# Chunked attention heads: the second copy of a query page's high half by a DMA from SP instead of by GpSimd

## The chip, the cores and the metric

The kernel runs on one core of a Trainium2 chip. Its engines are TensorE (PE; its weight loads are listed apart as PEld), VectorE (DVE), ScalarE (ACT), GpSimd (POOL) and SyncE (SP). Each runs its own list of instructions in order; semaphores order the lists against each other. In this kernel every DMA is issued by SP. The metric is the device time of one execution in microseconds.

## What is computed

One layer of a streaming encoder on a sequence of 1024 rows of width 1024, in float32:

```python
mod = silu(c) @ w_ada + b_ada                       # six rows of 1024: shift, scale, gate, twice
h = rmsnorm(x, g_attn_norm) * (1 + sc_a) + sh_a
proj = h @ w_in                                     # 416 latent columns, then q, k, v of 8 chunked heads
o_mla = latent attention, 8 heads, chunk-causal     # from the 416 columns
cq, ck, cv = rmsnorm(q), rmsnorm(k), v              # 8 heads of 64 columns
o_ca: each chunk of 64 queries sees its own and the 8 chunks before it;
      s = cq @ ck.T / 8 + rel_bias[clip(distance)]; softmax(s) @ cv
x = x + g_a * (concat(o_mla, o_ca) @ w_out)
h = rmsnorm(x, g_mlp_norm) * (1 + sc_m) + sh_m
gate, val = split(causal_dwconv(h @ w_up))
x = x + g_m * ((silu(gate) * val) @ w_down)
```

The change lies in `o_ca`, where the queries `cq` are brought into the form in which TensorE reads them.

## The kernel before

The 1024 rows are eight tiles of 128. To keep float32 accuracy on TensorE, an operand is split into a high part (rounded to fp32r) and a low part (what the rounding left), and a product is made from three matmuls: high by high, high by low and low by high.

The work goes in stages: the conditioning and the first projection (to about 85 us of the trace), the chunked heads together with the rest of the projections (to about 290 us, its last tiles to about 340), the latent heads (to about 600), the output projection, and the channel sub-layer, in which TensorE is busy with the up and down projections to the end.

The eight chunked heads come as four pairs p. A head pair's normalized queries and keys lie beside each other in a tile `qn` (128 rows, two heads of 64 query columns, two heads of 64 key columns). They are worked in two groups g of 512 queries, and in each group the two heads o follow each other, four query tiles of 128 each. So there are eight pages (p, g), each used by eight query tiles, and 64 query tiles in all.

`ca_pages(p, g)` makes a query page and a key page. TensorE transposes four blocks of `qn` into one PSUM bank (`page_psum`, L749): rows 0 to 63 hold head 0, rows 64 to 127 head 1. For each head o, ACT copies its 64 rows as the high part into `qp` (`qh[o]`, L781), DVE writes the low part into `qlow` (L782), and POOL copies the high part once more into the other 64 rows of the same tile (L783). The key page `kp` has the high part of the keys in head o's rows and their low part in the other 64 rows (L787 on ACT, L788 on DVE). One matmul over all 128 rows (L822 in `Unit.scores`) then makes high by high and high by low at once, and a second, with `qlow`, low by high. That is why the high part of the queries is needed twice.

`qfix[g]` holds two tiles (one for each head) for each group, so a page of pair p + 1 overwrites the tiles of the same group of pair p. The transposed queries and keys share one PSUM bank with one buffer: the key page is transposed after the query page has been read out.

A page is prepared two query tiles before its first use (the loop over `tiles`, `v.prep()`), where the projections it needs are done; else right before. The page of (p, o = 0) serves both heads: `ca_pages` runs once for a (p, g), and the tile of head 1 is used four query tiles after that of head 0.

A query tile goes through `scores` (TensorE, then DVE adds the bias and takes the row extreme, then ACT's exponential at L854, `Pc`), a normalization into two float16 halves `hlc` (POOL at L74 the high one, DVE at L876 the low one, both with the reciprocal `ric` from DVE), a DMA transpose issued by SP (L888, into `PTc`), and `values` (TensorE at L916). SP's list also holds the loads of weights (`wq_r`, `wv_r`, `wm_r` at L195, `aw` at L447), of biases (L946), and the stores of the output (`oT_d` at L930).

Between the attention tiles, TensorE is given steps of the other projections ("fillers"), paced by reckoned cost. The splits of those weights are on ACT (L78) and POOL (L85), and the normalization of the next pair's queries and keys (`qk_norm`: L350 to L357) ends on POOL with `qn`. The order of each engine's list is in the end set by a planner, which goes through the program with its own durations of each instruction and with priorities: scores, normalization and values are raised by fixed offsets (`OFF_S`, `OFF_P`, `OFF_V`). `issue_after` pins an instruction behind another on the same engine.

Of the kernel before, what the change touches and what calls it, by code (L numbers as in the profile page):

```python
# [65 lines left out]
def layer_kernel(ctx, tc, I, out):  # L66
    nc = tc.nc
    pe, act, dve, pool, sp = nc.tensor, nc.scalar, nc.vector, nc.gpsimd, nc.sync

    def f32(ap):  # L70
        return ap.bitcast(F32)
# [211 lines left out]
    for d in range(ND):  # L283
        dd, half = divmod(d, 2)
# [460 lines left out]
    def page_psum(src, name, rows, tag="T"):  # L745
        pt = ps.tile([P, 512], F32, name=f"{name}_ps", tag=tag, bufs=TB)
        with tc.issue_after(first[0]):
            for j in range(4):
                pe.transpose(pt[:rows, j * P:(j + 1) * P], src(j), ident[:])  # L749
        return pt  # L750
# [20 lines left out]
    def ca_pages(p, g):  # L771

        qn = qns[p, g]
        half = (slice(0, 64), slice(64, 128))
        pt = page_psum(lambda j: qn[:, j, 0:128], f"q{p}_{g}", P)
        if p == g == 0:
            pk_ = page_psum(lambda j: qn[:, j, 128:256], f"k{p}_{g}", P, "pv")
        qh = qfix[g]
        ql = qlow[0], qlow[1 + g]
        for o in range(2):  # L780
            act.activation(qh[o][half[o]], pt[half[o]], AF.Copy)  # L781
            dve.tensor_tensor(ql[o][half[o]], pt[half[o]], f32(qh[o][half[o]]), op=SUB)  # L782
            pool.tensor_copy(qh[o][half[1 - o]], f32(qh[o][half[o]]))  # L783
        pt = pk_ if p == g == 0 else page_psum(lambda j: qn[:, j, 128:256], f"k{p}_{g}", P)
        kk = kfix[(2 * p + g) % 3]
        for o in range(2):
            act.activation(kk[half[o], o], pt[half[o]], AF.Copy, scale=gk_ca[half[o]])  # L787
            dve.scalar_tensor_tensor(kk[half[1 - o], o], pt[half[o]], gk_ca[half[o]], f32(kk[half[o], o]),  # L788
                                     op0=MUL, op1=SUB)
        return (qh, ql), kk  # L790
# [165 lines left out]
    def ca_unit(p, g, o):  # L956
        def prep():
            if (p, g, o) == (0, 0, 0):
                load_bias(0)
            if g == 0 and o == 0:  # L960
                load_bias(2 * p + 1)
            if g == 1 and o == 0 and p < 3:
                load_bias(2 * p + 2)
            if g == 0:
                mask_bias(2 * p + o)
            if o == 0:
                pages["c", p, g] = ca_pages(p, g)
        u = Unit(f"c{p}{o}", 64 * o, 64,
                 lambda: (pages["c", p, g][0], [pages["c", p, i][1] for i in range(g + 1)]),
                 lambda j: vts[p][:, j, o].rearrange("p a b -> p (a b)"),  # L970
                 g, True, lambda: biases[2 * p + o], o, oT_d[4 + p], ("c", p // 2))
        u.prep = prep
        u.need = [f"qk{p}"] if p else []
        u.needv = [f"v{p // 2}"]
        return u
# [623 lines left out]
    for t in range(4):  # L1599
        o = dl.tile([P, 512], F32, name=f"oe{t}", tag="oe", bufs=3)  # L1600
# [80 lines left out]
```

## Time and profile before

| | |
|---|---|
| median of 3 runs | 1311.97 us (1311.38 to 1319.53) |
| the profiled execution | 1312.59 us, of which the trace's span is 1310.8 us |
| PE busy | 1189.1 us (91%) |
| DVE busy | 1075.0 us (82%) |
| ACT busy | 625.8 us (48%) |
| POOL busy | 597.9 us (46%) |
| all DMA of the program | 190.82 MB, mean 146 GB/s |

Busy times are of one execution under the profiler. A row of a group of instructions gives line, engine, operation, output and inputs by the names in the program, shape and count, then busy time and mean duration, then the idle time of that engine just before them and what ended it. A row of the timeline gives start, length, engine, line, operation, and in brackets the idle time before and its releaser; neighbours of one kind are merged with their count. Waits are rows "who waited <- for whom: us in total, times, longest". For a DMA, the duration is that of the issue on SP, and the time to landing is given apart. Idle time of an engine that isn't the bottleneck costs nothing by itself.

### The profile page before, as it was taken

Reading aid. Unit: us, or ns where it says so; the run is one execution under the profiler, and the core shown is the slowest. Engines: PE = TensorE matmul, PEld = TensorE weight load, DVE = VectorE, ACT = ScalarE, POOL = GpSimd, SP = SyncE. Lnnn points to the kernel's source line nnn. Section 1 sums busy time; section 2 is a strip of 40 time slices with the busy share of each in tenths; the row PEclk is TensorE's granted clock in tenths of the full one; section 3 lists DMA queues with packets and bytes.
Section 4 is the critical chain, followed back from the end, with each engine's and each line's share of the span. In section 5 each row is a group of like instructions: output and inputs, shape, how many; then the busy total and the mean of one; then the engine's idle time right before and its main releaser. Section 6 shows DMA issues by size and latency. Waiting matters only on the chain. (4 is left out here: it accounts for less than half of the span.)

```text
span 1310.8 us, 18660 instructions
## 1 busy us (share of the span) xinstructions
PE 1189.1 (91%) x6168; PEld 988.0 (75%) x6168; DVE 1075.0 (82%) x1800; ACT 625.8 (48%) x1148; POOL 597.9 (46%) x639
## 2 busy tenths in 40 slices
PE   3899998889767889878989999999999999999998
PEld 3789888878545667656778888888888886888886
DVE  6979988888589778875899889888888987687667
ACT  5454654455567454543474443444453353433331
POOL 5485773587688534445515444544445441000000
PEclk9899999989889998988999999999999999999999
DMA  8416758766224777679503333343333337943451
GB/s 323 150 50 154 177 141 189 158 161 123 51 70 85 161 162 149 147 161 357 231 0 112 97 125 116 119 128 107 105 121 111 122 105 267 395 135 102 129 161 64
DMA packets 223688, 190.82 MB, mean 146 GB/s; under 512 B 148708, under 2 KB 166372, under 8 KB 223592
## 3 DMA queue, kind: packets, MB, share of 16 engines
q1 hardware_dynamic: 223592, 189.64, 51.4%
q8 instruction: 48, 0.79, 0.3%
q14 instruction: 48, 0.39, 0.1%
HBM read 117.50 MB, written 37.49 MB: 118 GB/s over the span
## 5 line engine op out<-in xcount | busy, mean ns | idle before, releaser
L78 ACT ACTIVATE dnP<-dnr 128x1024 fp32r<-128x1024 f32 x73 | 77.5, 1065 | 116.3 <-PE dnA_P L1492 46.3
L1464 DVE TENSOR_TENSOR dnP<-dnr,dnP 128x1024 fp32r<-128x1024 f32 x72 | 88.3, 1230 | 51.3 <-ACT dnP L78 51.3
L74 POOL TENSOR_SCALAR hlm<-Pm,rim 128x512 f16<-128x512 f32 (+3 forms) x96 | 67.5, 712 | 73.4 <-DVE rim L857 20.2
L85 POOL TENSOR_TENSOR wf<-wu,wf 128x512 fp32r<-128x512 f32 x22 | 39.6, 1798 | 116.6 <-ACT wf L78 116.6
L85 POOL TENSOR_TENSOR wb<-wu,wb 128x512 fp32r<-128x512 f32 x22 | 43.8, 1993 | 84.8 <-ACT wb L78 57.1
L876 DVE SCALAR_TENSOR_TENSOR hlm<-Pm,rim,hlm 128x512 f16<-128x512 f32 (+3 forms) x96 | 72.3, 769 | 12.4 <-POOL hlm L74 12.1
L829 PE MATMUL sm<-kp,qp 96*128 96x512 f32 (+7 forms) x288 | 70.0, 370 | 10.8 <-ACT Pm L854 7.7
L1326 DVE SCALAR_TENSOR_TENSOR u<-c,cvp,u 128x1023 f32<-128x1023 f32 x44 | 55.8, 1310 | 27.6 <-ACT u L1325 26.2
L854 ACT ACTIVATE Pm<-sm,mm 128x128 f32<-128x128 f32 (+3 forms) x64 | 47.3, 740 | 44.7 <-DVE mm L847 35.4
L74 POOL TENSOR_SCALAR hlc<-Pc,ric 128x640 f16<-128x640 f32 (+2 forms) x64 | 48.8, 765 | 42.8 <-DVE ric L857 14.7
L854 ACT ACTIVATE Pc<-sc,mc 128x640 f32<-128x640 f32 (+2 forms) x64 | 42.3, 662 | 51.4 <-DVE mc L844 28.6
L829 PEld LDWEIGHTS sm<-kp,qp 96*128 96x128 f32 (+1 forms) x288 | 48.0, 195 | 21.9 <-ACT Pm L854 12.3
L1325 ACT ACTIVATE u<-c,cvp 128x1024 f32<-128x1024 f32 x44 | 52.4, 1240 | 23.4 <-DVE c L1424 16.5
L916 PE MATMUL pvm<-PTm,vt 128*128 128x256 f16 (+1 forms) x320 | 42.6, 279 | 19.7 <-DMA PTm<-hlm 17.1
L876 DVE SCALAR_TENSOR_TENSOR hlc<-Pc,ric,hlc 128x640 f16<-128x640 f32 (+2 forms) x64 | 52.5, 827 | 8.5 <-POOL hlc L74 8.3
L78 ACT ACTIVATE wc<-ws 128x512 fp32r<-128x512 f32 x21 | 13.3, 634 | 92.9 <-DVE ws L1174 87.1
L1327 DVE SCALAR_TENSOR_TENSOR u<-c,cvp,u 128x1022 f32<-128x1022 f32 x44 | 55.5, 1302 | 0.0
L155 PE MATMUL ipq<-wq_s,hT 128*128 128x256 f32 x192 | 55.5, 289 | 0.0
L916 PEld LDWEIGHTS <-vt 128*128 128x128 f16 x320 | 30.1, 103 | 33.3 <-issue 20.5
L157 PE MATMUL ipq<-wq_s,hT 128*128 128x256 f32 x192 | 54.6, 284 | 0.0
L156 PE MATMUL ipq<-wq_s,hT 128*128 128x256 f32 x192 | 54.6, 284 | 0.0
L1491 PE MATMUL dnA_P<-dnP 128*128 128x512 f32 x132 | 51.3, 389 | 0.0
(436 smaller groups left out, 4376.0 us busy)
## 6 DMA issues: line engine op xcount, KB each, us to landing
wu<-w_up SPq DMA_DIRECT2D x44, 512.0 KB, 3.6
dnr<-g_d SPq DMA_DIRECT2D x73, 256.0 KB, 2.8
aw<-w_ada SPq DMA_DIRECT2D x48, 256.0 KB, 3.2
g_d<-u SPq DMA_DIRECT2D x22, 512.0 KB, 3.0
dnr<-w_down SPq DMA_DIRECT2D x44, 256.0 KB, 5.4
adaw<-w_ada_a SPq DMA_DIRECT2D x16, 512.0 KB, 6.4
x<-x SPq DMA_DIRECT2D x16, 512.0 KB, 9.1
g_d<-gs SPq DMA_DIRECT2D x22, 256.0 KB, 2.8
```

The lines of the kernel that those rows point to most:

```text
L74: pool.tensor_scalar(o, i, s, 1.0, op0=MUL, op1=MUL)
L78: act.activation(o, i, AF.Copy)
L85: (pool if eng == "p" else dve).tensor_tensor(o, i, f32(hi), op=SUB)
L155: pe.matmul(pt, sh, mh, start=(start and i == 0), stop=False)
L156: pe.matmul(pt, sh, ml, start=False, stop=False)
L829: last = pe.matmul(s[:, c:c + w], qpg[a][rr, q], kpgs[kh][rr, b, ko:ko + w], start=(a == 0 and b == 0), stop=(a == 1))
L854: act.activation(pr[:, :n], sv, AF.Exp, bias=m[:], scale=-1.0, accum_out=rsum[:, 0:1])
L876: dve.scalar_tensor_tensor(hl[:, w:2 * w], pp, ri[:], hl[:, :w], op0=MUL, op1=SUB)
L916: last = pe.matmul(dst, u.vst(j), mov, start=(x == 0), stop=(x == len(todo) - 1), skip_group_check=True)
L1326: dve.scalar_tensor_tensor(u[:, 1:], c[:, :S - 1], cvp[:, cv + 1:cv + 2], u[:, 1:], op0=MUL, op1=ADD)
L1327: dve.scalar_tensor_tensor(u[:, 2:], c[:, :S - 2], cvp[:, cv:cv + 1], u[:, 2:], op0=MUL, op1=ADD)
L1464: r = f(*a, **k)
```

## The change

For seven of the eight pages, the copy of the high part into the other 64 rows is a DMA within SBUF, issued by SP. The first page (p = 0, g = 0) keeps POOL's copy. Source, destination and bytes are the same: 64 rows of 512 float32, 128 KB. There are two copies for each page, so 14 instructions leave POOL's list and 14 DMAs come into SP's.

```diff
         for o in range(2):
             act.activation(qh[o][half[o]], pt[half[o]], AF.Copy)
             dve.tensor_tensor(ql[o][half[o]], pt[half[o]], f32(qh[o][half[o]]), op=SUB)
-            pool.tensor_copy(qh[o][half[1 - o]], f32(qh[o][half[o]]))
+            if p == g == 0:
+                pool.tensor_copy(qh[o][half[1 - o]], f32(qh[o][half[o]]))
+            else:
+                sp.dma_start(f32(qh[o][half[1 - o]]), f32(qh[o][half[o]]))
```

## The prediction

> **What bounds the kernel now.** I read the page's busy table first, then a table of windows by stage, then what TensorE (PE) waited for in the stage that the change touches.
>
> ```profile
> span 1310.8 us, 18660 instructions
> PE 1189.1 (91%) x6168; PEld 988.0 (75%) x6168; DVE 1075.0 (82%) x1800; ACT 625.8 (48%) x1148; POOL 597.9 (46%) x639
> 85.00:290.00 205.00, 183.69 (x1386) 170.47 (x1386) 182.00 (x516) 108.27 (x268) 131.06 (x169) 0.97 0.68 159
> 290.00:600.00 310.00, 254.56 (x1364) 200.25 (x1363) 240.54 (x558) 167.33 (x401) 186.69 (x252) 0.92 0.61 129
> 750.00:1310.00 560.00, 551.66 (x2403) 451.35 (x2401) 457.19 (x458) 231.88 (x288) 160.52 (x106) 0.99 0.43 141
> ```
>
> The last three rows are start:end, length, then busy time and count of PE, PE's weight loads, DVE, ACT and POOL, then granted clock, DMA share and GB/s. After 750 us PE is nearly full (551.66 of 560) and nothing of this change reaches it. The copies of the change stand between 85 and 290 us: there PE is busy 183.69 of 205 and DVE 182.00, so two engines are close to the limit and POOL, with 131.06, is not. PE leaves 205 - 183.69 = 21.3 us idle in that stage; this is all that the change could win there. Who took it:
>
> ```profile
> PE pvc L916 <- DMA PTc<-hlc: 9.6, 7, 2.5
> PE sc L822 <- ACT Pc L854: 7.4, 6, 2.7
> ```
>
> (us in total, times, longest.) PE waits for transposed probabilities, which SP's DMA queue brings, and for a score bank that ACT's exponential frees. It never waits for the POOL copy, as its own rows say:
>
> ```profile
> L783 POOL CAST qp<-qp 64x512 fp32r<-64x512 f32 x16 | 10.9, 680 | 9.8 <-ACT qp L781 9.0
> 85.20 1.28 POOL L783 CAST qp<-qp 64x512 fp32r<-64x512 f32 x2
>   POOL hlc L74: 0.2, 1
> ```
>
> The first is the group of all 16 copies (busy us, mean ns, POOL idle before them and its releaser), the second the pair that the change keeps, the third the only instruction that waited for a copy.
>
> **Removed from POOL.** 14 copies go: 10.9 - 1.28 = 9.6 us of POOL, and its 9.0 us of waiting for ACT, which all stand before the 14. Whether that is worth anything depends on what stood behind each copy:
>
> ```profile
> 142.13 0.61 POOL L783 CAST qp<-qp 64x512 fp32r<-64x512 f32 x1 [4.24 <-ACT qp L781]
> 142.97 0.84 POOL L74 TENSOR_SCALAR hlc<-Pc,ric 128x640 f16<-128x640 f32 x1 [0.23 <-POOL qp L783]
> 142.66 0.15 DVE L857 TENSOR_SCALAR ric<-ric 128x1 f32<-128x1 f32 x1
> 269.06 0.61 POOL L783 CAST qp<-qp 64x512 fp32r<-64x512 f32 x1
> 269.75 1.21 POOL L85 TENSOR_TENSOR wm_l<-wm_r,wm_h 128x160 fp32r<-128x160 f32 x2
> 271.70 1.05 POOL L357 TENSOR_TENSOR qn<-raw,r 128x512 f32<-128x512 f32 x1
> ```
>
> At the longest wait (4.24) the next POOL instruction needed DVE's `ric`, ready at 142.81, so it could start only 0.16 us sooner. At 269 the copy does stand in a chain: it holds the line up by 269.75 - 269.06 = 0.7 us, and at the end of that line is the normalization `qn` of the last rows of pair 3, which the key page of that pair is made from. PE's score there is the only one of the stage with a wait for a key page:
>
> ```profile
> 274.83 0.33 PE L822 MATMUL sc<-kp,qp 128*128 128x128 f32 x1 [0.32 <-DVE kp L788]
> ```
>
> So this copy's going is worth between 0.3 (what PE waited) and 0.7 us; I take 0.7. At the other places POOL's next work waits for ACT or DVE, or PE is full; nothing.
>
> There is also DVE. Instructions with two inputs in SBUF stretch at times:
>
> ```profile
> L461 DVE SCALAR_TENSOR_TENSOR aacc<-aw,cs,aacc x42: 674/751/1415, 114.0 to 297.4; 128x512 f32<-128x512 f32 x42
> L461 DVE SCALAR_TENSOR_TENSOR aacc<-aw,cs,aacc 128x512 f32<-128x512 f32 x39 | 33.3, 853 | 2.9 <-DMA aw<-w_ada 2.6
> ```
>
> Shortest 674 ns, mean in the stage 853: 39 x 179 ns = 7.0 us more than the shortest. If overlap with POOL does that, the copies' part of it is 9.6 of POOL's 131.06, or 0.5 us; with the other groups of two SBUF inputs I take 1.0 us. Bounds: nothing, and 14 x 0.68 = 9.5 us, if every copy blocked DVE for its whole length.
>
> The Trainium skill, page "SBUF — State Buffer", section "SBUF: two separate sides", says that VectorE instructions with two SBUF inputs and GpSimd instructions that read SBUF exclude each other for the whole instruction, and that DMA has other ports. The stretched rows agree with it without proving it; by the rule in full, DVE's gain is the upper bound just given, which is the mechanism of the faster rival below.
>
> **Added to SP.** 14 DMAs of 64 rows x 2 KB, 128 KB each. No row shows SBUF to SBUF without a transpose; the nearest is the store of attention output, also 64x512 out of SBUF and also issued by SP. Beside it the transposes that share SP:
>
> ```profile
> L930 SPq DMA_DIRECT2D oT_d<-oc x16: 451/461/667, 109.3 to 339.7; - x16
> DMA to landing us min/median/max: 2.2/2.3/3.1
> L888 SPq DMA_TRANSPOSE PTc<-hlc x64: 1167/1314/2634, 93.1 to 332.5; - x64
> DMA to landing us min/median/max: 2.4/3.4/5.6
> PTc<-hlc SPq DMA_TRANSPOSE x42, 3.4
> ```
>
> I take 0.46 us of issue and 2.3 us to landing; upper ends are the store's 0.67 of issue and the slowest transpose's 5.6. From the end of ACT's `qp` to a usable copy that is 2.8 us, at worst 6.3, where POOL needed 0.6 plus its own queue. The tightest three of the 14:
>
> ```profile
> 266.43 0.60 ACT L781 ACTIVATE qp<-q_ps 64x512 fp32r<-64x512 f32 x1
> 163.11 0.58 ACT L781 ACTIVATE qp<-q_ps 64x512 fp32r<-64x512 f32 x1
> 171.68 0.80 PE L822 MATMUL sc<-kp,qp 128*128 128x512 f32 x1
> 269.36 0.59 ACT L781 ACTIVATE qp<-q_ps 64x512 fp32r<-64x512 f32 x1
> 279.67 0.33 PE L822 MATMUL sc<-kp,qp 128*128 128x128 f32 x1
> ```
>
> Source ready to first use: 267.03 to 274.83 is 7.8 us, 163.69 to 171.68 is 8.0, 269.95 to 279.67 is 9.7; the other eleven have 13 us and more. The work that hides the landing is the two score tiles between a page's preparation and its use; that cover lasts until SP is more than 7.8 - 2.8 = 5.0 us late (1.5 us with the worst landing). I cost the latency at nothing.
>
> What isn't hidden is SP's order. Fourteen issues are 14 x 0.46 = 6.4 us of SP. In 130 to 290 us SP issues 42 transposes, and PE waited for seven of them in the stage; if 14/42 of these stand behind a new DMA, PE loses 7 x 1/3 x 0.46 = 1.1 us. And the new DMA waits for ACT in SP's queue, with transposes, weight loads and output stores behind it, and PE, ACT and DVE behind those. Bounds: nothing, and the 9.0 us that the same wait cost POOL. SP has slack of its own:
>
> ```profile
> SPq L888 <- DVE hlc L876: 26.1, 12, 4.5
> ```
>
> that is 26.1 us in 12 waits of transposes for DVE, in the same stage, so most of a wait for ACT falls where the next transpose isn't ready either. I take 1.0 us, near the lower end, as three of POOL's four waits held nothing up.
>
> The Trainium skill, "DMA: Bandwidth & Descriptors", section "Queues, rings and completion order", speaks against the change: all that SP issues goes through one ring per DMA engine, and descriptors are taken in ring order, so a transpose also stands behind the copy's data. An estimate of that with the stage's 159 GB/s at a 0.68 share, or 234 GB/s when busy: 128 KB is 0.56 us, again on a third of seven, 1.3 us more, which would make 1313 of the sum. The traces of before show no copy to test it on.
>
> **Sum.** -0.7 (key page of pair 3) - 1.0 (DVE) + 1.1 (issue) + 1.0 (waits in SP's queue) = +0.4 us. Against the profiled execution, 1312.59 us (span 1310.8 and 1.8 around it), this is 1313.0; that execution lies 0.6 above the median shown, 1311.97, so 1312.4 on that scale. I say 1312. Its own range is 1306 to 1318: 6 us either way is about a quarter of the stage's 21.3 us of idle PE.
>
> **Rivals.** Faster: DVE is the stage's second bound, and gets back up to 9.5 us; with PE's 7.4 us of waiting for ACT's exponential (itself behind DVE) and the 0.7 gone, 1312 - 8 = 1304, at most 1302 with DVE's full 9.5. For it: DVE busy 182.00 of 205. Against: that share of the stretch gave 1 us, not 9.5.
>
> Slower: the copy's wait moves from POOL, where little stood behind it, to SP, where the transposes stand, and PE's largest wait is for these. All 9.0 us on PE's path: 1312 + 9 = 1321. It decides wherever SP reaches the DMA before ACT has run `qp` and a transpose behind it has its data; over 5.0 us late, the scores of the three tight pages are late as well, some 2 us each, up to 1327. Against it are SP's own 26.1 us of waiting for DVE.
>
> Another order: each queue's order comes from a planner that reckons with its own durations. A longer copy and an emptier POOL may move weight splits, projections and scores between 90 and 600 us. No row prices that. The stages up to 600 us leave 21.3 and 310 - 254.56 = 55.4 us idle; I bound it by a quarter of their sum, 19 us, either way.
>
> Not what it says: POOL keeps its copies, or SP's DMAs stand so late that PE waits each time. The first would give 1312.
>
> **How the numbers follow.** Forecast 0.46 (all within 1%). Faster rival 0.16, about a third of it beyond 1%: 0.05. Slower rival 0.24, half beyond 1%: 0.12, as its price of 1321 to 1327 lies about that edge. Another order 0.13: 0.05 faster, 0.03 within, 0.05 slower. Not what it says 0.01. One per cent is 13 us, about what a measurement of this kernel can tell from no change. Together faster 0.10, same 0.46 + 0.11 + 0.12 + 0.03 + 0.01 = 0.73, slower 0.17. The range, 1301 to 1325, takes in the faster rival's and most of the slower one's price.
>
> **What would show it.** Right: two copies left on POOL, 14 DMAs on SP with issue near 0.46 us and landing under 3.5; no PE wait for a `qp` DMA above 0.5 us; PE's wait for `PTc` in 85 to 290 us within 3 us of 9.6, its busy time near 183.7, POOL's near 121. Wrong: transposes waiting for ACT `qp` in SP's queue by several us, or a stage boundary (the start of the run after 750 us) moved by more than 6 us with the copies nowhere on the path, which would be the planner's order.

## The result, and the profile after

The median of the changed kernel is 1318.34 us (1314.53 to 1323.07 in 20 runs), that of the kernel before, in runs beside it, 1314.22 us (1308.59 to 1321.92 in 20). The ratio is 1.0036 with a 95% interval of 1.0020 to 1.0051: slower by about 4.7 us, a small effect that stands clear of zero. Measured again later (`e9_change_again`) it was 1.0028 (1.0013 to 1.0043).

The profiled execution of after took 1322.2 us, near the top of its runs, and that of before 1312.59, in the lower half of its own. The 9.6 us between the two traces are therefore about twice what the medians show; sizes are taken from the ratios, and the traces are read for places. The span and the busy row of the page of after:

```profile
span 1320.4 us, 18642 instructions
PE 1193.1 (90%) x6168; PEld 991.7 (75%) x6168; DVE 1065.9 (81%) x1800; ACT 623.7 (47%) x1148; POOL 587.3 (44%) x625
```

POOL has 14 instructions fewer and 10.6 us less to do, and DVE, whose instructions are the same 1800, is 9.1 us less busy (1075.0 before); the second trace of the same kernel (`e9`) has 1072.9, so most of that doesn't repeat. PE has the same 6168 matmuls and is busy 4.0 us longer. The stages, in the windows of after (start:end, length, busy time and count of PE, PE's weight loads, DVE, ACT and POOL, then granted clock, DMA share, GB/s):

```profile
85.00:290.00 205.00, 182.78 (x1374) 169.41 (x1372) 172.13 (x504) 104.55 (x255) 115.87 (x143) 0.96 0.71 163
290.00:600.00 310.00, 253.79 (x1360) 201.94 (x1360) 236.63 (x566) 164.72 (x407) 189.16 (x261) 0.90 0.59 124
750.00:1310.00 560.00, 556.88 (x2421) 455.72 (x2420) 457.85 (x456) 237.65 (x297) 163.72 (x109) 0.99 0.43 141
```

The second row is the one to look at. PE is as busy as before (253.79 against 254.56), but its granted clock is 0.90 where it was 0.92. How far behind the kernel is at the end of attention, the first matmul of the output projection says; this is its group in before, and then in after (duration in ns shortest/median/longest, first and last start in us, forms):

```profile
L155 PE MATMUL op<-wo,oh x64: 389/389/792, 596.3 to 644.3; 128*128 128x512 f32 x64
```

```profile
L155 PE MATMUL op<-wo,oh x64: 387/389/796, 604.9 to 651.7; 128*128 128x512 f32 x64
```

Of the 9.6 us between the traces, 604.9 - 596.3 = 8.6 are there by the end of attention. The copies themselves, first in the instructions of the tile `qp`, then in those of the changed line with the time from issue to landing:

```profile
L786 SPq DMA_DIRECT2D qp<-qp x14: 467/485/1541, 88.6 to 292.9; - x14
L784 POOL CAST qp<-qp x2: 607/609/611, 85.1 to 85.8; 64x512 fp32r<-64x512 f32 x2
```

```profile
DMA to landing us min/median/max: 2.2/3.0/4.4
```

PE has no wait for one of these DMAs anywhere in the trace. What it did wait for in 85 to 290 us (us in total, times, longest):

```profile
PE sc L825 <- ACT Pc L857: 10.6, 9, 3.1
PE pvc L919 <- DMA PTc<-hlc: 7.4, 6, 3.3
```

The two waits sum to 18.0 us, where they were 9.6 + 7.4 = 17.0. And SP's queue in the same stretch:

```profile
SPq L891 <- DVE hlc L879: 21.8, 13, 3.9
...
SPq L786 <- ACT qp L781: 5.3, 3, 4.6
...
SPq L786 <- ACT v L423: 3.4, 1, 3.4
```

The wait for ACT has moved from POOL (9.0 us) to SP (5.3 and 3.4), and SP's wait for DVE has shrunk from 26.1 us. DVE's stretched group of that stage has fewer and shorter instructions than before (us, mean ns, idle before them):

```profile
L461 DVE SCALAR_TENSOR_TENSOR aacc<-aw,cs,aacc 128x512 f32<-128x512 f32 x35 | 28.1, 803 | 8.6 <-DMA aw<-w_ada 8.2
```

A mean of 803 ns stands against 853; that 35 of the 42 are in the window and not 39 is the later stage. The mean says little about the copies: with POOL's copies in the order of after (`e2`, below) it is 807, and in the four kernels below that keep the old order and have 12 or 14 of POOL's copies fewer it is 832 to 837. So where the copies alone go, some 18 ns of 853 go with them, about 0.7 us in all, near the 0.5 that the prediction took for this group; the rest of the 50 ns comes with the order.

By the chunk stage's own rows the change does about what was forecast: PE has done 12 matmuls fewer by 290 us (1374 against 1386). Yet the kernel is 4.7 us slower.

One more comparison points to the place. Leaving the copies out, and taking each engine's instructions (by line, operation and tile) from the traces in order of time, the longest sequence that both kernels have in common holds 5589 of PE's 6168 matmuls, 1424 of DVE's 1800 instructions, 999 of ACT's 1143, 548 of POOL's 623 and 610 of SP's 682. The first place that differs is at 91 us (DVE), the last at 656 (PE): from the start of the chunked heads to just behind the output projection. The change gave the planner another engine and another operation for 14 copies, and it has ordered that stretch anew.

### The profile page after: what moved, and what is told of

It is laid out like the page before. It is cut to its first block, busy times and chain, and to the rows that moved or that the text cites. A ratio compares the mean times of both kernels' runs of the same rounds, so it can differ in the third digit from the quotient of the medians.

```text
span 1320.4 us, 18642 instructions
## 1 busy us (share of the span) xinstructions
PE 1193.1 (90%) x6168; PEld 991.7 (75%) x6168; DVE 1065.9 (81%) x1800; ACT 623.7 (47%) x1148; POOL 587.3 (44%) x625
## 4 chain that ended last, share of the span: by engine, by line
PE 56%; DVE 10%; POOL 4%; issue 4%; DMA 4%; ACT 2%; SPq 1%; POOLq 0%; ACTq 0%; DVEq 0%
PE p L1158 10%; PE p L1160 10%; PE p L1159 10%; PE dnA_P L1493 2%; PE dnA_P L1494 2%; PE dnA_P L1495 2%; DMA PTm<-hlm 2%; DVE hlm L879 2%; PE sm L832 2%; PE dnB_P L1494 2%; PE dnB_P L1495 2%; PE dnB_P L1493 2%; PE pvm L919 1%; POOL ur L121 1%; DVE mm L850 1%
## 5 line engine op out<-in xcount | busy, mean ns | idle before, releaser
L74 POOL TENSOR_SCALAR hlm<-Pm,rim 128x512 f16<-128x512 f32 (+2 forms) x96 | 66.3, 701 | 61.8 <-ACT Pm L857 17.1
L1329 DVE SCALAR_TENSOR_TENSOR u<-c,cvp,u 128x1023 f32<-128x1023 f32 x44 | 56.3, 1321 | 27.6 <-ACT u L1328 26.2
L879 DVE SCALAR_TENSOR_TENSOR hlm<-Pm,rim,hlm 128x512 f16<-128x512 f32 (+2 forms) x96 | 68.2, 726 | 7.9 <-POOL hlm L74 7.8
L879 DVE SCALAR_TENSOR_TENSOR hlc<-Pc,ric,hlc 128x640 f16<-128x640 f32 (+2 forms) x64 | 49.5, 779 | 11.5 <-POOL hlc L74 11.3
L850 DVE TENSOR_REDUCE mm<-sm 128x1 f32<-128x128 f32 (+3 forms) x64 | 47.2, 747 | 11.5 <-PE sm L832 11.1
```

The lines of the kernel that those rows point to most:

```text
L74: pool.tensor_scalar(o, i, s, 1.0, op0=MUL, op1=MUL)
L850: anchor["dve"] = dve.tensor_reduce(m[:], sv, axis=AX.X, op=MIN).ins
L879: dve.scalar_tensor_tensor(hl[:, w:2 * w], pp, ri[:], hl[:, :w], op0=MUL, op1=SUB)
```

## The experiments

Two theories stood against each other. **The DMA**: the wait and the issue in SP's queue cost the 4.7 us. **The order**: the DMA costs next to nothing, and what costs is the planner's new order of everything else. To part them, the order of each engine's instructions can be pinned: before the planner runs, dependencies of order alone are added from each instruction to the next of its engine, by a stored list, the copies left free. The traces show that it holds: leaving the copies out, `e1`, `e3`, `e11` and `e12` have the sequence of before on every engine without exception, and `e2` and `e10` that of after. The kernels with a pinned order below contain this (shortened, with a comment added):

```diff
+COPIES = set()
+def pin_order(tc):
+    plain = [i for i in tc.nc.cur_bb.bb.instructions if i.name not in COPIES]
+    for steps in json.loads(zlib.decompress(base64.b64decode(ORDER))):
+        n, prev = 0, None
+        for s in steps:
+            n += s
+            if prev is not None:
+                tc.add_manual_dep(plain[n], prev.name, ...)   # order alone, no semaphore
+            prev = plain[n]
```

The ratios are to the kernel before on the same chip, with 95% intervals. Kernels e1 to e4, e5 to e8 and e9 to e12 shared a chip each.

**The DMA in the old order.** The 14 copies are DMAs of SP as in the change; all other instructions keep the order of before.

```diff
-                sp.dma_start(f32(qh[o][half[1 - o]]), f32(qh[o][half[o]]))
+                COPIES.add(sp.dma_start(f32(qh[o][half[1 - o]]), f32(qh[o][half[o]])).ins.name)
...
+        pin_order(tc)                              # ORDER: that of before
```

> The 14 DMAs in place of POOL's copies, but every other instruction of all five engines pinned to the order of the kernel before; only the DMAs' own places in SP's list are the planner's. If the DMAs themselves cost the time (SP's issue, its waits for ACT, the landing), the whole +4.7 us of the change appears here: ratio about 1.0036 to the kernel before. If the planner's new order of the other instructions costs it, this is within 1.5 us of the kernel before: 0.999 to 1.001, and a little faster if DVE's and POOL's relief is worth something (down to 0.997).

Measured: 1313.51 us, ratio 1.0009 (0.9989 to 1.0028). Without the re-ordering, the change costs nothing that this measurement can tell from zero; up to 3.7 us isn't excluded. The rows of the changed line, and then what PE waited for in 85 to 290 us:

```profile
L786 SPq DMA_DIRECT2D qp<-qp x14: 467/482/1731, 88.6 to 293.9; - x14
```

```profile
PE pvc L919 <- DMA PTc<-hlc: 8.5, 6, 2.5
PE sc L825 <- ACT Pc L857: 8.0, 11, 1.9
```

Issue as in after; PE's two waits sum to 16.5 us against 17.0 in before.

**POOL copies in the new order.** The reverse: the copies stay on POOL, everything else stands in the order of after.

```diff
-                sp.dma_start(f32(qh[o][half[1 - o]]), f32(qh[o][half[o]]))
+                COPIES.add(pool.tensor_copy(qh[o][half[1 - o]], f32(qh[o][half[o]])).ins.name)
...
+        pin_order(tc)                              # ORDER: that of after
```

> POOL's copies of the kernel before, with every other instruction pinned to the order of the changed kernel. If the order costs the time: ratio about 1.0036 to the kernel before. If the DMAs do: 0.999 to 1.001.

Measured: 1321.30 us, ratio 1.0078 (1.0055 to 1.0101). The order alone, with no DMA in it, is slower than before, by more than was expected and by more than the whole change. The first matmul of the output projection comes at 603.7 us, as late as in after (604.9), while it was at 594.4 in `e1`.

**The new order and the change, again, side by side.** The changed kernel as it is, and the kernel of `e2` once more, on one chip.

> The changed kernel once more, beside the next one, so that DMA and POOL copies are compared in the same order and on the same chip. From its first comparison: ratio 1.002 to 1.005 to the kernel before. If DMA or POOL makes no difference in a given order, as in the order of before (1.0009), it agrees with the next one within 2 us.

> POOL's copies in the order of the changed kernel, a second time; the first gave 1.0078 (1.0055 to 1.0101), above the changed kernel's 1.0036. If the DMA is better in the order that was planned for it: 4 us or more above the run before this one. If not, within 2 us of it.

Measured: 1316.68 us, ratio 1.0028 (1.0013 to 1.0043), for the change, and 1320.30 us, ratio 1.0056 (1.0036 to 1.0077), for POOL copies in its order. So within the new order the DMA is the better copy, by 3.6 us of median (the intervals overlap a little), a little less than the 4 us that were named as the sign of it. What the order costs therefore depends on the copy. With POOL's copies it is 0.56 to 0.78%, 7 to 10 us, clear of zero twice; but that order was planned for DMAs, and POOL's copies may fit it badly. With the DMAs it is the distance from `e1` (1.0009) to the change (1.0036 and 1.0028), some 2.5 to 3.5 us, with intervals that overlap. The order is shown to cost; that nothing of the 4.7 us is the DMA's isn't shown.

**No copy for pairs 1 to 3, old order.** The 12 copies of pairs 1 to 3 are left out; the other halves keep the queries of pair 0.

```diff
-            else:
-                sp.dma_start(f32(qh[o][half[1 - o]]), f32(qh[o][half[o]]))
+            elif p == 0:
+                COPIES.add(pool.tensor_copy(qh[o][half[1 - o]], f32(qh[o][half[o]])).ins.name)
```

> For pairs 1 to 3 the second copy is left out altogether (12 of the 16; the matmuls read the rows of pair 0 there), all else in the order of the kernel before. It shows what freeing POOL, and DVE with it, can be worth at most. If my 1.7 us (0.7 for the key page of pair 3, 1.0 for DVE) is right: ratio 0.998 to 0.9995. If DVE gets back up to 9.5 us and passes it on: 0.993 to 0.996. If nothing waits for POOL: 0.9995 to 1.0005.

Measured: 1315.51 us, ratio 1.0018 (1.0000 to 1.0037). The gain expected of freeing POOL isn't there; the ratio lies above all three of the expected ranges. The windows of this kernel show that the work did go:

```profile
85.00:290.00 205.00, 184.85 (x1394) 172.90 (x1393) 179.41 (x511) 108.58 (x268) 121.64 (x156) 0.96 0.69 158
```

POOL is busy 121.64 us there instead of 131.06, and DVE 179.41 instead of 182.00; PE did not use it.

**A copy on ACT, planner's own order.** ACT writes the second half straight from PSUM; the planner orders as it likes.

```diff
-                sp.dma_start(f32(qh[o][half[1 - o]]), f32(qh[o][half[o]]))
+                act.activation(qh[o][half[1 - o]], pt[half[o]], AF.Copy)
```

> The second copy made by ACT, from PSUM straight into the other 64 rows, for the seven pages; order by the planner. ACT gets 14 x 0.59 = 8.3 us more of 108 busy in 205, POOL loses 9.6; no DMA, no wait for the first copy. If where the copy stands matters little and each new order moves the time by some us at random: anywhere in 0.995 to 1.005. If SP's queue is what costs, this is free of it: 0.996 to 1.000.

Measured: 1325.63 us, ratio 1.0101 (1.0078 to 1.0123). That is slower than either expectation. It adds 14 copies of 0.59 us to ACT, and it gets an order of its own as well (1388 of DVE's 1800 instructions are in the order of before), so by itself it doesn't say which of the two costs.

**Another order for no reason.** The kernel before, POOL copies and all; only the constant by which the kernel paces the fillers among the chunked heads moves by 1%, and with it the order.

```diff
-R_CA, R_MLA = 1.9, 0.5
+R_CA, R_MLA = 1.88, 0.5        # the other run: 1.92
```

> The kernel before with POOL's copies, and one pacing constant of the chunked stage changed from 1.90 to 1.88 (how much projection work is put between score tiles). The work is the same, instruction for instruction; only the planner's order differs, by about as much as that of the changed kernel. If any other order costs some us because the order of before is a lucky one: ratio 1.002 to 1.010. If orders are scattered about that of before: 0.996 to 1.004, and the change's order is an unlucky one. If what the planner does with SP's DMAs is special: 0.999 to 1.001 here.

> As the one with 1.88, with 1.92. The same three answers: 1.002 to 1.010 if the order of before is a lucky one, 0.996 to 1.004 if orders scatter about it, 0.999 to 1.001 if only the DMAs make the planner's order bad.

Measured: 1320.25 us, ratio 1.0063 (1.0039 to 1.0088), and 1330.07 us, ratio 1.0147 (1.0120 to 1.0174). With no change to any operation, two more orders are slower by 0.6% and 1.5%, the second by more than expected. With the order of after, and that of `e4` (whose time also holds its copies), all four new orders are on the slow side: the order of before looks like a good one among its neighbours, though four are few.

**Where in the order.** POOL copies; in the first kernel the order is that of after up to the first score of the last head pair (at some 275 us) and that of before behind it, in the second the other way round.

> POOL's copies; all instructions up to the first score of pair 3 (about 275 us) in the order of the changed kernel, from there on in that of the kernel before. In the trace with the new order and POOL's copies, scores are 4 us late at that point and 6 to 8 us late at 306 to 332 us. If the loss is made in the end of the chunked stage and behind it: ratio 0.999 to 1.002. If it is made before 275 us: 1.004 to 1.008.

> The other way round: the order of the kernel before up to the first score of pair 3, then that of the changed kernel, POOL's copies throughout. If the loss is made in the end of the chunked stage and behind it: ratio 1.005 to 1.008. If before 275 us: 0.999 to 1.003.

Measured: 1315.97 us, ratio 1.0028 (1.0013 to 1.0042), and 1316.81 us, ratio 1.0040 (1.0025 to 1.0055). Neither expectation holds: both halves cost, together 0.68%, about what the whole order costs with POOL's copies (0.78 and 0.56%). So the loss isn't made on one side of 275 us alone.

**Twice the load on SP.** Old order; behind each copy, SP issues a second DMA of the same rows, to a buffer in DRAM that nobody reads.

```diff
+                COPIES.add(sp.dma_start(spare_d[2 * (2 * p + g) + o], f32(qh[o][half[o]])).ins.name)
```

> Order of the kernel before, the 14 DMAs, and behind each one a second DMA of the same 64 rows to a spare place in DRAM that nothing reads: SP's issues and the data in its rings doubled, no new wait for a result. If SP's issues and data cost what I reckoned (1.1 us, and 1.3 more by the ring): ratio 1.0015 to 1.003. If SP's queue has room: 0.999 to 1.0015, as with one DMA (1.0009).

Measured: 1316.63 us, ratio 1.0032 (1.0015 to 1.0049). Against `e1` (1.0009, another chip) that is 0.23%, 3 us, for 14 more issues and their data, though the two intervals overlap. The added line's instructions and then PE's waits in 85 to 290 us:

```profile
L788 SPq DMA_DIRECT2D spare_d<-qp x14: 451/587/904, 88.9 to 304.3; - x14
```

```profile
PE sc L827 <- ACT Pc L859: 10.7, 10, 2.9
PE pvc L921 <- DMA PTc<-hlc: 9.9, 9, 2.8
```

The waits sum to 20.6 us against `e1`'s 16.5, at the transposes and the score bank, where the prediction looked for the price of a DMA in SP's queue. That is one trace of each, though, and this sum doesn't rank the kernels: it is 13.6 in `e4`, among the slowest, and 12.2 in `e8`.

**The DMA issued by ACT.** Old order; the same 14 DMAs, issued by the engine that makes their source, so that nothing in SP's queue waits for it.

```diff
-                sp.dma_start(f32(qh[o][half[1 - o]]), f32(qh[o][half[o]]))
+                COPIES.add(act.dma_start(f32(qh[o][half[1 - o]]), f32(qh[o][half[o]])).ins.name)
```

> Order of the kernel before, the 14 DMAs issued by ACT, right in the list that makes their source, instead of by SP. ACT gets 14 issues of about half a us, SP's list is that of the kernel before. If the waits and issues in SP's list cost anything: below the 1.0009 of SP's DMAs, 0.997 to 1.000. If ACT's issues stand in the way of the exponentials: 1.002 to 1.005.

Measured: 1309.60 us, ratio 0.9966 (0.9949 to 0.9983). This version beats both kernels, by 4.2 us of median that of before beside it. The rows of the changed line, then PE's waits in 85 to 290 us:

```profile
L786 ACTq DMA_DIRECT2D qp<-qp x14: 468/468/502, 88.8 to 289.4; - x14
...
DMA to landing us min/median/max: 2.3/2.6/4.7
```

```profile
PE sc L825 <- ACT Pc L857: 7.8, 6, 2.9
PE pvc L919 <- DMA PTc<-hlc: 7.1, 5, 3.2
```

The longest issue is 0.502 us where SP's was 1.731, and PE's two waits sum to 14.9 us, against 15.9 to 20.6 in the other kernels that have the old order throughout. ACT pays 14 x 0.468 = 6.6 us of issue out of an idle half of its time. That SP's queue is what it saves may be, but isn't shown: `e3`, which has the same order, no DMA copies and only two copies more on POOL than this one, is slower than it by 0.52% (other chips), so kernels of one order lie that far apart for reasons that these runs don't show.

**What the new order does to PE.** The stretch from the end of the chunked heads into the latent heads, 320 to 430 us, as the windows show it, in before, `e1`, after and `e2`, in this order:

```profile
320.00:430.00 110.00, 84.07 (x398) 62.76 (x396) 85.83 (x214) 70.03 (x190) 88.94 (x113) 0.91 0.34 74
```

```profile
320.00:430.00 110.00, 84.46 (x405) 63.28 (x404) 85.59 (x214) 71.17 (x194) 89.35 (x115) 0.91 0.32 73
```

```profile
320.00:430.00 110.00, 80.58 (x382) 60.58 (x381) 81.09 (x211) 65.12 (x178) 84.87 (x113) 0.88 0.31 68
```

```profile
320.00:430.00 110.00, 82.50 (x386) 62.39 (x385) 80.66 (x212) 65.38 (x179) 83.99 (x115) 0.86 0.32 68
```

The first two have the old order, the last two the new one, whichever engine copies: in the new order PE gets through 382 and 386 matmuls in place of 398 and 405, at a lower granted clock. The other traces agree: the five with the new order in this stretch (`e8`, `e9` and `e10` too) have 379 to 386 matmuls, the six with the old one (`e3`, `e7`, `e11` and `e12` too) 395 to 411. Over the whole run, the profiled executions show this:

| kernel | order | span, us | PE busy, us | mean clock |
|---|---|---|---|---|
| before | old | 1310.8 | 1189.1 | 0.969 |
| `e1` | old | 1308.6 | 1185.6 | 0.973 |
| `e3` | old | 1308.4 | 1187.0 | 0.970 |
| `e12` | old | 1309.3 | 1188.2 | 0.970 |
| after | new | 1320.4 | 1193.1 | 0.962 |
| `e9` | new | 1318.5 | 1191.4 | 0.961 |
| `e2` | new | 1318.7 | 1194.6 | 0.958 |
| `e10` | new | 1317.2 | 1189.5 | 0.962 |

The means are 1309.3 and 1187.5 us for the old order, 1318.7 and 1192.2 for the new: of 9.4 us of span, half (4.7) is longer busy time for the same matmuls, and the other half is idle PE. The 9.4 is too much: by the ratios the two groups are 0.5% apart, some 7 us, and the profiled executions of before, `e1` and `e3` lie low among their own runs. (`e11`, in the old order, had 1317.7 us and 0.965 in a profile at the top of its runs.) The clock holds over all runs, not the profiled ones alone: its mean is 0.967 to 0.971 in `e1`, `e3`, `e11` and `e12`, and 0.959 to 0.964 in after, `e9`, `e2` and `e10`.

## Why the prediction was right, and where it was not

The forecast of 1312 us, a change of +0.4, against a measured ratio of 1.0036: by that ratio the median shown at the start, 1311.97, becomes 1316.7 us, inside the range of 1301 to 1325 and inside the forecast's own range of 1306 to 1318. Within 1% was the likeliest case, and it came. But the size is about 4.3 us off, and no term of the sum made the time that was measured: the number fell into the range by the range's width, which was set for other reasons. What was right is that PE waits for no copy; what was missed is what they do to the order. Nor does the prediction have a term for the clock: it counts idle PE alone, where about half of the difference between the traces is longer busy time.

- **What bounds the stage**: held. PE's two waits stayed about what they were (18.0 us in sum against 17.0), and PE waited for no copy.
- **Issue**, 14 x 0.46: 0.485 us at the median, 0.467 at the least. The longest took 1.541, at 94.9 us right behind two transposes, which the upper end of 0.67 didn't hold.
- **Landing and its cover**: 2.3 us taken, 3.0 measured (4.4 at most, under the bound of 5.6). The cover of 7.8 us was enough; costing the latency at nothing held.
- **Waits in SP's queue**, 1.0 us of bounds 0 to 9.0, and **issue on PE's path**, 1.1: no run has them alone. `e1` holds both, and came out at 1.0009 (0.9989 to 1.0028), that is -1.4 to +3.7 us; +0.4 lies in it. Doubling the DMAs cost some 3 us more, and taking them off SP won 0.43% (`e12` against `e1`, other chips). So the price in SP's queue may be real and larger than the 2.1 us; with `e3` where it is, these runs don't settle it. The estimate by the ring, 1.3 us more, isn't settled by them either.
- **-0.7 for the key page of pair 3 and -1.0 for DVE**: not seen. `e3`, with 12 of the 14 copies gone and nothing in their place, was 1.0018 (1.0000 to 1.0037), not faster. DVE got back little: against 1075.0 us of busy time in before, the old order with the copies off POOL has 1072.7 (`e1`), 1074.0 (`e3`), 1075.5 (`e11`) and 1070.7 (`e12`). The 9.1 us of after look like the upper bound of 9.5, but the same kernel has 2.1 in `e9`, and `e2`, with all of POOL's copies, has 5.0. So the faster rival's mechanism at its full size isn't borne out here, and the 1.0 us lies within the scatter of these traces. It was wrong to pass it on to PE: in after, whose trace has the lightest DVE, PE's wait for the score bank rose to 10.6 us.
- **Another order by the planner**, chance 0.13: this is what happened. The sign that was named for it, a stage boundary moved by more than 6 us with the copies nowhere on the path, is in the trace, and `e1` and `e2` show it by exchanging order and copy. Two things were wrong about it. Its chance was too low: both changes of the copy that left the planner free (after, `e4`), and both of the pacing, came out in another order. And its sign was left even, where four new orders in four came out slower (0.6 to 1.5% with POOL copies or a changed constant, 1.0% with ACT's). Its bound of 19 us held for this change; of the others, `e6` (1.0147, 19.3 us) lies just past it.
- **The slower rival** (SP's head of the line, 1321 to 1327): not the cause. Its mechanism may be there in small (`e11`, `e12`), but `e1` rules out its price of 9 us.

What stays open: why `e12` is faster than `e3`, which leaves 12 of the 14 copies out altogether. By the ratios that is 0.52%, and freeing POOL and DVE can't explain it, as `e3` has that too. Nor is it shown which moves in the new order lose the time: both halves of it do. In the traces of after, `e2`, `e9` and `e10`, the matmul with the number of the one that starts at 290 us in before starts 0.1 to 2.1 us later, that of 341 us 6.5 to 8.5 us later, and the output projection's first 7.1 to 8.6 us later. So most of the lag is made behind 290 us, as idle PE and clock and not as one wait. How much of the change's 4.7 us is the order and how much the DMA is open within the intervals given above.

## What to carry to other kernels

Where a planner orders the instructions, a change of one operation is two changes: pin the old order and measure the operation alone, and measure a placebo (a pacing constant moved by 1%) before crediting or blaming the operation. A DMA that waits for an engine's result can be issued by that engine if it has time to spare: here that was the fastest version, though why isn't shown. Take a second trace before believing a busy time: the same kernel had 9.1 and 2.1 us less on DVE. Busy time taken from an engine that isn't the bound is no gain until some wait of the bound is seen to shrink.

## What the runs showed of the hardware

A copy of 64 x 512 float32 from SBUF to SBUF by DMA was issued in 0.47 us at the least on SP and on ACT alike (up to 1.73 on SP, in `e1`) and landed in 2.2 to 4.7 us, at the median 2.6 (`e12`) to 3.5 (`e1`). The store of the same size to DRAM in before landed in 2.3 at the median.

Longer busy time for the same matmuls, at a lower granted clock, made about half of the loss in the traces. Four windows of 10 us in `e9` show how (PE's busy time comes first, the clock stands behind the busy times):

```profile
330.00:340.00 10.00, 7.34 (x50) 6.00 (x48) 5.35 (x14) 3.95 (x13) 9.18 (x20) 0.98 0.60 95
340.00:350.00 10.00, 5.13 (x22) 3.74 (x23) 2.54 (x6) 4.01 (x8) 5.91 (x10) 0.50 0.53 131
350.00:360.00 10.00, 8.59 (x31) 6.06 (x29) 5.83 (x19) 4.66 (x14) 3.01 (x5) 0.83 0.00 1
360.00:370.00 10.00, 7.84 (x30) 4.86 (x29) 6.50 (x18) 6.27 (x18) 8.23 (x9) 1.00 0.00 1
```

PE is idle for half of the second window, and the clock there is 0.50; in the third it is busy again at 0.83, and only the fourth is at full speed. The Trainium skill, page "TensorE: Matmul & The Clock Gate", section "Part 1: The HAM clock gate (the "warmup" mystery)", says that the gate halves the clock after an idle window of about 3.4 us and opens again after a busy one. The traces agree with the length: by their clock records, each stretch at half clock lasts 3.4 us or a multiple of it, up to 20.5 (but for the last, which the end cuts off). But the window needn't be wholly idle, as before shows at 270 us:

```profile
266.00:268.00 2.00, 1.80 (x8) 1.34 (x8) 2.00 (x4) 1.34 (x3) 1.83 (x3) 1.00 0.54 136
268.00:270.00 2.00, 0.24 (x2) 0.00 (x0) 1.62 (x6) 1.01 (x2) 1.85 (x3) 0.99 1.14 183
270.00:273.40 3.40, 3.29 (x17) 2.80 (x18) 2.20 (x4) 1.31 (x4) 3.33 (x5) 0.50 0.61 159
273.40:276.00 2.60, 1.83 (x10) 1.28 (x9) 1.88 (x7) 2.03 (x5) 2.52 (x5) 1.00 0.75 177
```

PE was idle for 1.8 of two microseconds and busy right before, and the clock was halved for the next 3.4. PE was busy for 3.29 of these, and behind them the clock is at 1.00 again.

The idle gap of `e9` isn't new with the order. Before has it too, a little earlier:

```profile
330.00:340.00 10.00, 5.01 (x32) 3.51 (x29) 2.79 (x4) 4.88 (x13) 7.95 (x15) 0.74 0.55 132
340.00:350.00 10.00, 8.64 (x30) 6.56 (x30) 5.78 (x20) 6.07 (x16) 3.55 (x4) 0.75 0.06 13
350.00:360.00 10.00, 8.48 (x32) 5.33 (x32) 7.68 (x20) 6.38 (x18) 8.22 (x11) 1.00 0.00 0
```

By the clock records, 10.2 us at half speed follow there, and 13.7 in `e9`. Over the run it is 73 to 84 us in before, `e1`, `e3` and `e12`, and 101 to 113 in after, `e9`, `e2` and `e10`. So where an order lengthens a gap, the loss is paid twice, as the gap and as slow matmuls behind it.
